# GLA scores as two half-row products per direction in two PSUM banks, with both spreads of q on ScalarE

## The chip, the cores and the metric

The kernel runs on one core of one Trainium2 chip. The metric is the device time of one execution in microseconds. Five engines work side by side: TensorE (PE; its weight loads are listed apart as PEld), VectorE (DVE), ScalarE (ACT), GpSimd (POOL) and SyncE (SP), which issues most of the DMAs. An engine runs its own instructions in the order in which they were written out and waits on semaphores for the others.

## What is computed

Two layers work on 1024 latent and 256 context tokens, 1280 in all, of width 1024. In each layer one input projection feeds four mixers: GLA (gated linear attention), neighbourhood attention (NA), a diagonal state space model (S5) and pooling. Their outputs go through gates and one output projection. The change touches GLA alone, which has 4 heads with keys of 32 and values of 64 and runs over the tokens forward and backward; the two results are added:

```python
def step(state, inp):
    qc, kc, vc, gc = inp
    b = jnp.cumsum(gc, axis=-2)
    diff = b[:, :, :, None, :] - b[:, :, None, :, :]
    decay = jnp.exp(jnp.where(lower[:, :, None], diff, -jnp.inf))
    att = jnp.einsum('bhid,bhjd,bhijd->bhij', qc, kc, decay)
    o = (jnp.einsum('bhij,bhje->bhie', att, vc)
         + jnp.einsum('bhid,bhde->bhie', qc * jnp.exp(b), state))
    b_last = b[:, :, -1:, :]
    state = (jnp.exp(b_last)[:, :, 0, :, None] * state
             + jnp.einsum('bhjd,bhje->bhde', kc * jnp.exp(b_last - b), vc))
    return state, o
...
o + flip_seq(gla_chunked(flip_seq(qh), flip_seq(kh), flip_seq(vh), flip_seq(log_gate(gb, 1)), s_b))
y = o * lax.rsqrt(jnp.mean(o * o, axis=-1, keepdims=True) + NORM_EPS) * g
```

`att` is what this document calls the scores: for each head a product over its 32 key channels.

## The kernel before

**Tiling.** The 4 heads' 32 key channels lie side by side on the 128 partitions, so that QF and KF (forward) and QB and KB (backward), with the decay already worked into them, are tiles of 128 channels by 1280 tokens. GLA goes over the tokens in chunks of 128, of which there are ten. Layer 0 needs scores for all ten. Layer 1 is the last, needs no output for the 256 context tokens, and makes scores for eight, so 18 chunks have scores.

**The two loops.** `gla` first runs the backward loop. For each chunk it scales the state into `glSb` (L1040, VectorE) and updates the state: a transpose of KB on TensorE (L934), a copy to `kt` on ScalarE (L936), a product with `vt` on TensorE (L938), and two VectorE operations (L1031 to `km`, L1032 to `S`). Then the forward loop runs. For each chunk:

- The spread (`gla_spread`): to keep the heads apart in one product over all 128 partitions, q is written four times side by side into `qs` [128, 4, 128], and in copy h the channels of the other heads are set to zero. The forward q is spread by four ScalarE instructions (L971), the backward q by one GpSimd instruction over 512 columns (L973).
- The scores (L1062): one matmul for each direction, K as the weights and 512 columns of `qs` streaming, into one bank of PSUM from the pool `pb`. All of it is float32, which TensorE runs in two passes, so each matmul stands in the profile as two.
- The masks, both VectorE, PSUM to SBUF: the forward scores times a mask into `at` (L1065), then the backward ones over it where they belong (L1067).
- `gla_finish`: forward state times QF (L946), `at` times `vt` for four heads (L948), backward state times QB (L950), all into one bank; a square on ScalarE (L953), a sum (L955), an inverse square root in a row of [128, 4] operations (L132 to L140) and a scaling (L957) on VectorE, two transposes on TensorE (L960), a copy out on ScalarE (L962) and a DMA.
- The forward state's update (L934 to L938, L1031, L1032).

**What sets the order.** GLA, the S5 projection, NA's projections (L318, L334), the modulation (L198) and later the pooling's projection and the gates are written one after the other, the latter three marked as later. A scheduler with priorities works out each engine's order when the kernel is built: where GLA waits for another engine, TensorE is given matmuls of the later work, which this document calls fillers. Pools set what can be open at once: `pb` has 5 banks of PSUM in GLA, `qs` two buffers, `at` two. After S5, a branch splits the program; no filler crosses it. The other way of computing GLA behind that branch isn't executed.

Of the kernel before, what the change touches and what calls it, by code (L numbers as in the profile page):

```python
# [50 lines left out]
BD = 'ap'  # L51
ATB = 2
QSB = 2
# [17 lines left out]
class Kernel:  # L71
# [893 lines left out]
    def gla_spread(self, out, Q, ind, d):  # L965

        nc = self.nc
        sh = [128, 4, 128]
        if BD[d] == "a":
            for h in range(4):  # L970
                nc.scalar.activation(out[:, h], Q, AF.Copy, scale=ind[:, h:h + 1])  # L971
        else:
            (nc.gpsimd if BD[d] == "p" else nc.vector).tensor_tensor(out, Q.unsqueeze(1).to_broadcast(sh), ind.unsqueeze(2).to_broadcast(sh), ALU.mult)  # L973

    BWD = [1, 0] + list(range(NT - 1, 1, -1))

    def gla(self, l, last):
# [7 lines left out]
        with self.phase("glF", True):  # L985
# [28 lines left out]
            with self.phase("glm"):  # L1014
# [3 lines left out]
                ind = self.t([128, 4], "ind1", 1)  # L1018
# [33 lines left out]
                for c in range(NT):  # L1052
                    cs = slice(c * 128, (c + 1) * 128)
                    vt = self.gla_load_v(l, c)
                    if not (last and c < 2):
                        at = self.t([128, 4, 128], "at", ATB)
                        sh = [128, 4, 128]
                        for d, (K, Q) in enumerate(((KF, QF), (KB, QB))):
                            qs = self.t(sh, "qs", QSB)
                            self.gla_spread(qs, Q[:, cs], ind, d)  # L1060
                            ps = self.pb()
                            nc.tensor.matmul(ps, lhsT=K[:, cs], rhs=qs.rearrange("p h i -> p (h i)"), start=True, stop=True)  # L1062
                            pv = ps.rearrange("p (h i) -> p h i", h=4)
                            if d == 0:
                                v.tensor_tensor(at, pv, mf.unsqueeze(1).to_broadcast(sh), ALU.mult)  # L1065
                            else:
                                v.copy_predicated(at, mb.unsqueeze(1).to_broadcast(sh), pv)  # L1067
                        sf = turned(S, 0, c, self.t([128, 256], "Sft", 2))
                        self.gla_finish(l, c, vt, lambda h: at[:, h, :], QF[:, cs], sf, QB[:, cs], Sb[:, c, :], gn)
                    if c != NT - 1:  # L1070
                        S = state(0, KF, vt, c, S)
# [444 lines left out]
    def run(self):  # L1516
# [9 lines left out]
        for l in range(DEPTH):  # L1526
# [5 lines left out]
            with self.phase("mods", True) as pool:  # L1532
# [3 lines left out]
                self.npb = 5  # L1536
# [44 lines left out]
def _consts():  # L1581
# [33 lines left out]
    out["ind1"] = (ind > 0).astype(f)  # L1615
# [110 lines left out]
```

## Time and profile before

| | us |
|---|---|
| median of 3 runs | 1388.77 |
| the runs | 1386.04 to 1389.81 |
| the profiled execution | 1390.5 |
| its span in the trace | 1388.7 |

| engine | busy us | share of the span |
|---|---|---|
| PE | 1265.2 | 91% |
| DVE | 912.5 | 66% |
| ACT | 584.9 | 42% |
| POOL | 203.8 | 15% |

GLA's two loops run from about 228 to 366 us in layer 0 and from about 930 to 1047 us in layer 1. A wait of TensorE there adds to the time unless a later wait swallows it; a wait of another engine does so only where TensorE then waits for it. In the timelines below a group's length holds the modelled end of its last pass; what a pass takes is read from the start of one group to the start of the next.

### The profile page before, as it was taken

To read this page: it belongs to the slowest core of one execution; us is meant where nothing else is said; L and a number is where in the kernel's file an instruction comes from. 1 tells how busy PE (TensorE), PEld (TensorE's weight loads), DVE (VectorE), ACT (ScalarE), POOL (GpSimd) and SP (SyncE) were. 2 spreads that over 40 slices of the span, in tenths; PEclk is the share of its full clock that TensorE was granted. 3 is DMA by queue.
4 is the path that set the end of the run, shared out by engine and by line. 5 is a ranking of instruction groups with operands and counts; after the bars stand their busy time and mean duration, and the time that the engine had idled before them with its cause. 6 is when DMAs were issued, how large, how long until landed. Compare 5 with 4: busy or idle time off the path is not lost. (4 is left out here: it accounts for less than half of the span.)

```text
span 1388.7 us, 20066 instructions
## 1 busy us (share of the span) xinstructions
PE 1265.2 (91%) x6958; PEld 1011.0 (73%) x6958; DVE 912.5 (66%) x2269; ACT 584.9 (42%) x1218; POOL 203.8 (15%) x212
## 2 busy tenths in 40 slices
PE   5799999999999999988989999999899998777897
PEld 2698967667777678767878989768667776665676
DVE  2777577456388548773866787586654884776383
ACT  2653443223333347663555644443323333665321
POOL 0100000001100024351410000000112100234220
PEclk9699999999999999999999999999999999998999
DMA  9436685752533267746832475865215535754662
GB/s 330 157 116 224 192 252 166 217 182 76 164 127 113 81 184 197 209 141 208 246 124 92 124 230 188 246 183 157 79 46 185 166 108 161 201 150 139 192 210 91
DMA packets 223477, 231.07 MB, mean 166 GB/s; under 512 B 47016, under 2 KB 176552, under 8 KB 223040
## 3 DMA queue, kind: packets, MB, share of 16 engines
q1 hardware_dynamic: 221776, 227.14, 53.8%
q10 hardware_dynamic: 1584, 2.49, 0.5%
q8 instruction: 58, 0.95, 0.3%
q14 instruction: 59, 0.48, 0.1%
HBM read 159.97 MB, written 69.62 MB: 165 GB/s over the span
## 5 line engine op out<-in xcount | busy, mean ns | idle before, releaser
L318 PE MATMUL pa<-ahi,wh 128*128 128x512 f32 (+1 forms) x664 | 171.7, 387 | 5.0 <-ACT stg L1407 2.1
L318 PE MATMUL pa<-alo,wh 128*128 128x512 f32 (+1 forms) x664 | 166.9, 380 | 0.1
L318 PE MATMUL pa<-ahi,wl 128*128 128x512 f32 (+1 forms) x664 | 165.1, 377 | 0.1
L318 PEld LDWEIGHTS pa<-ahi,wh 128*128 128x128 f32 x664 | 116.0, 193 | 31.8 <-issue 6.4
L318 PEld LDWEIGHTS pa<-alo,wh 128*128 128x128 f32 x664 | 115.7, 192 | 25.7 <-issue 7.9
L318 PEld LDWEIGHTS pa<-ahi,wl 128*128 128x128 f32 x664 | 115.6, 191 | 23.5 <-issue 5.5
L334 PE MATMUL pa<-wh,ahi 128*128 128x256 f32 (+1 forms) x480 | 83.4, 305 | 5.8 <-ACT wh L302 2.4
L303 POOL TENSOR_TENSOR wl<-w,wh 128x1024 fp32r<-128x1024 f32 (+1 forms) x19 | 46.3, 2441 | 286.0 <-PE pa L318 170.8
L388 PE MATMUL po<-wx,ahi 128*128 128x512 f32 x312 | 79.8, 396 | 1.1 <-DVE stg L474 1.0
L334 PE MATMUL pa<-wl,ahi 128*128 128x256 f32 (+1 forms) x480 | 79.6, 299 | 0.1
L1315 PE MATMUL nS<-naK,naQ 128*128 128x256 f32 (+2 forms) x256 | 61.2, 359 | 19.8 <-DVE nast L1322 17.8
L302 ACT CAST wh<-w 128x1024 fp32r<-128x1024 f32 (+1 forms) x51 | 53.8, 1057 | 58.8 <-PE pa L318 36.4
L334 PEld LDWEIGHTS pa<-wh,ahi 128*128 128x128 f32 x480 | 68.8, 197 | 11.4 <-issue 3.3
L334 PE MATMUL pa<-wh,alo 128*128 128x256 f32 (+1 forms) x480 | 76.0, 294 | 0.0
L334 PEld LDWEIGHTS pa<-wl,ahi 128*128 128x128 f32 x480 | 68.1, 195 | 6.6 <-issue 5.3
L1315 PEld LDWEIGHTS nS<-naK,naQ 128*128 128x128 f32 x256 | 46.0, 209 | 32.9 <-DVE nast L1322 28.1
L388 PEld LDWEIGHTS po<-wx,ahi 128*128 128x128 f32 x312 | 59.2, 191 | 14.7 <-DVE stg L474 1.4
L334 PEld LDWEIGHTS pa<-wh,alo 128*128 128x128 f32 x480 | 65.7, 193 | 5.7 <-issue 5.5
L1322 DVE CUSTOM_DVE_ANT_0 naP<-nS,nab 128x640 f32<-128x640 f32 (+1 forms) x64 | 50.3, 787 | 24.3 <-PE nS L1315 12.0
L1327 ACT ACTIVATE naP<-naP,nast 128x640 f32<-128x640 f32 (+1 forms) x64 | 51.5, 805 | 25.1 <-DVE nast L1322 22.3
L1382 PE MATMUL nT<-naPT,naV 128*128 128x256 f32 (+3 forms) x368 | 53.4, 284 | 7.9 <-DVE naPT L1367 5.4
L973 POOL TENSOR_TENSOR qs<-QB,ind 128x512 f32<-128x512 f32 x18 | 19.2, 1066 | 275.4 <-PE pb L1062 159.8
(395 smaller groups left out, 2601.6 us busy)
## 6 DMA issues: line engine op xcount, KB each, us to landing
wm<-in_w_mod_dram SPq DMA_DIRECT2D x48, 512.0 KB
w<-in_w_in_dram SPq DMA_DIRECT2D x41, 512.0 KB
s5R<-dR SPq DMA_DIRECT2D x16, 960.0 KB
xt<-in_tok_dram SPq DMA_DIRECT2D x20, 512.0 KB
dR<-sp_R SPq DMA_DIRECT2D x16, 512.0 KB
dG<-stg SPq DMA_DIRECT2D x32, 256.0 KB
w<-in_w_out_dram SPq DMA_DIRECT2D x16, 512.0 KB
naQ<-dQ SPq DMA_DIRECT2D x24, 320.0 KB
```

What stands on the lines that cost most here:

```text
L302: nc.scalar.copy(hi, raw)
L303: (next(engines) if engines else self.eng(2)).tensor_tensor(lo, raw, hi.bitcast(F32), ALU.subtract)
L318: nc.tensor.matmul(ps[:, :t1 - t0], lhsT=w(k), rhs=x[:, k, t0:t1], start=(i == 0), stop=(i == 23))
L334: nc.tensor.matmul(ps[:, :n], lhsT=x[:, k, t * 128:(t + 1) * 128], rhs=w(k), start=(i == 0), stop=(i == 23))
L388: self.nc.tensor.matmul(o, lhsT=x[:, k], rhs=m(k), start=first and i == 0, stop=last and i == len(todo) - 1)
L973: (nc.gpsimd if BD[d] == "p" else nc.vector).tensor_tensor(out, Q.unsqueeze(1).to_broadcast(sh), ind.unsqueeze(2).to_broadcast(sh), ALU.mult)
L1315: nc.tensor.matmul(ps[:, c * 128:(c + n) * 128], lhsT=Qb[:, i, :], rhs=K[:, b * 128:(b + n) * 128], start=(i == 0), stop=(i == 1))
L1322: v.tensor_tensor_reduce(P[:, 0:nk], ps, bias[:, b0:b0 + nk], 1.0, -NEG, ALU.add, ALU.min, nm)
L1327: nc.scalar.activation(P[:, 0:nk], src, AF.Exp, bias=nm, scale=-1.0, accum_out=l1)
L1382: nc.tensor.matmul(out[:, q:q + n], lhsT=w, rhs=x, start=(i == 0), stop=(i == len(todo) - 1))
```

## The change

The heads are taken in two halves of TensorE's rows: heads 0 and 1 on partitions 0 to 63, heads 2 and 3 on partitions 64 to 127. `qs` becomes [128, 2, 128]: copy 0 keeps the even head of each half, copy 1 the odd one. A direction's scores are then two matmuls (L1059), one for each half: 64 rows of K as the weights, 256 columns of `qs` streaming, at rows 0 and 64 of the array. The two halves write to different banks of one new tile `sc` [128, 1024], which has a single buffer; each bank holds the forward and the backward scores of two heads. The masks (L1064, L1065) are still two VectorE operations, now over both banks. Both directions are spread by ScalarE (L967), two instructions each, so four a chunk as before; GpSimd has no spread left. `pb` has 3 banks in GLA where it had 5, which makes room for `sc`.

```diff
-BD = 'ap'
...
-    def gla_spread(self, out, Q, ind, d):
-
-        nc = self.nc
-        sh = [128, 4, 128]
-        if BD[d] == "a":
-            for h in range(4):
-                nc.scalar.activation(out[:, h], Q, AF.Copy, scale=ind[:, h:h + 1])
-        else:
-            (nc.gpsimd if BD[d] == "p" else nc.vector).tensor_tensor(out, Q.unsqueeze(1).to_broadcast(sh), ind.unsqueeze(2).to_broadcast(sh), ALU.mult)
+    def gla_spread(self, out, Q, ind):
+
+        for h in range(2):
+            self.nc.scalar.activation(out[:, h], Q, AF.Copy, scale=ind[:, h:h + 1])
...
-                ind = self.t([128, 4], "ind1", 1)
+                ind = self.t([128, 2], "ind1", 1)
...
-                        sh = [128, 4, 128]
+
+                        ps = self.ps2.tile([128, 1024], F32, tag="sc", bufs=1, name=self.nm("sc"))
+                        pd = ps.rearrange("p (b d n) -> p d b n", b=2, d=2)
                         for d, (K, Q) in enumerate(((KF, QF), (KB, QB))):
-                            qs = self.t(sh, "qs", QSB)
-                            self.gla_spread(qs, Q[:, cs], ind, d)
-                            ps = self.pb()
-                            nc.tensor.matmul(ps, lhsT=K[:, cs], rhs=qs.rearrange("p h i -> p (h i)"), start=True, stop=True)
-                            pv = ps.rearrange("p (h i) -> p h i", h=4)
-                            if d == 0:
-                                v.tensor_tensor(at, pv, mf.unsqueeze(1).to_broadcast(sh), ALU.mult)
-                            else:
-                                v.copy_predicated(at, mb.unsqueeze(1).to_broadcast(sh), pv)
+                            qs = self.t([128, 2, 128], "qs", QSB)
+                            self.gla_spread(qs, Q[:, cs], ind)
+                            for b in range(2):
+                                hp = slice(64 * b, 64 * b + 64)
+                                nc.tensor.matmul(pd[:, d, b], lhsT=K[hp, cs], rhs=qs[hp].rearrange("p h i -> p (h i)"), start=True, stop=True)
+                        av = at.rearrange("p (b h) i -> p b h i", b=2)
+                        sh = [128, 2, 2, 128]
+                        every = lambda m: m.unsqueeze(1).unsqueeze(1).to_broadcast(sh)
+                        pv = pd.rearrange("p d b (h i) -> p d b h i", h=2)
+                        v.tensor_tensor(av, pv[:, 0], every(mf), ALU.mult)
+                        v.copy_predicated(av, every(mb), pv[:, 1])
...
-                self.npb = 5
+                self.npb = 3
...
-    out["ind1"] = (ind > 0).astype(f)
+    out["ind1"] = (ind[:, 0:2] + ind[:, 2:4] > 0).astype(f)
```

Line numbers of the kernel after are a few smaller: L933, L935 and L937 are the transpose, the copy and the product of the state's update (L934, L936 and L938 before), L945, L947 and L949 the three products of `gla_finish`, L959 its transposes, L317, L333 and L197 the fillers.

The scheduler moves work. TensorE in the backward loop of layer 0, before: the updates' pairs L938 and L934 with fillers L334 (`pa`) between them, then the first chunk's scores.

```order
L938 MATMUL pb_1801<-vt_1795,kt_1799 128x256
L934 MATMUL pb_1810<-c_ident,KB_1563 128x128
L334 MATMUL pa_3261<-wl_3205,ahi 128x256
L334 MATMUL pa_3261<-wl_3211,ahi 128x256 x3
L938 MATMUL pb_1814<-vt_1808,kt_1812 128x256
L934 MATMUL pb_1823<-c_ident,KB_1563 128x128
L334 MATMUL pa_3261<-wl_3211,ahi 128x256
L334 MATMUL pa_3261<-wh_3204,alo 128x256 x3
L938 MATMUL pb_1827<-vt_1821,kt_1825 128x256
L1062 MATMUL pb_1842<-qs_1837,KF_1561 128x512
L1062 MATMUL pb_1847<-qs_1845,KB_1563 128x512
L946 MATMUL pb_1852<-Sft_1850,QF_1560 128x256
```

TensorE there now. `sc` are the half-row scores, of the first chunk and then of the second.

```order
L937 MATMUL pb_1725<-vt_1719,kt_1723 128x256
L933 MATMUL pb_1732<-c_ident,KB_1563 128x128
L1059 MATMUL sc_1837<-qs_1838,KF_1561 128x256
L937 MATMUL pb_1736<-vt_1730,kt_1734 128x256
L933 MATMUL pb_1745<-c_ident,KB_1563 128x128
L1059 MATMUL sc_1837<-qs_1838,KF_1561 128x256
L937 MATMUL pb_1749<-vt_1743,kt_1747 128x256
L933 MATMUL pb_1758<-c_ident,KB_1563 128x128
L1059 MATMUL sc_1837<-qs_1843,KB_1563 128x256 x2
L317 MATMUL pa_3172<-ahi,wh_3098 128x512 x2
L317 MATMUL pa_3172<-alo,wh_3098 128x512 x7
L937 MATMUL pb_1762<-vt_1756,kt_1760 128x256
```

The scores of the first chunks have moved up among the updates, in the places of fillers, and the two halves of a direction are in part apart.

ScalarE in the same loop, before: `kt` are the copies that the updates need, `qs` the forward spreads, of which the first chunk's come ahead of the loop and the next after it.

```order
L936 COPY kt_1734<-pb_1732 128x128
L936 COPY kt_1747<-pb_1745 128x128
L936 COPY kt_1760<-pb_1758 128x128
L936 COPY kt_1773<-pb_1771 128x128
L1199 CAST stn_3197<-pa_3172 128x8x8x8
L936 COPY kt_1786<-pb_1784 128x128
L936 COPY kt_1799<-pb_1797 128x128
L1218 CAST stg_3241<-pa_3216 128x4x64
L936 COPY kt_1812<-pb_1810 128x128
L936 COPY kt_1825<-pb_1823 128x128
L971 ACTIVATE qs_1895<-QF_1560,ind_361_1713 128x128 x4
```

ScalarE there now.

```order
L967 ACTIVATE qs_1838<-QF_1560,ind_361_1713 128x128 x2
L967 ACTIVATE qs_1843<-QB_1562,ind_361_1713 128x128 x2
L935 COPY kt_1734<-pb_1732 128x128
L935 COPY kt_1747<-pb_1745 128x128
L967 ACTIVATE qs_1896<-QF_1560,ind_361_1713 128x128 x2
L935 COPY kt_1760<-pb_1758 128x128
L967 ACTIVATE qs_1901<-QB_1562,ind_361_1713 128x128 x2
L935 COPY kt_1773<-pb_1771 128x128
L935 COPY kt_1786<-pb_1784 128x128
L967 ACTIVATE qs_1956<-QF_1560,ind_361_1713 128x128 x2
L935 COPY kt_1799<-pb_1797 128x128
L967 ACTIVATE qs_1961<-QB_1562,ind_361_1713 128x128 x2
```

Both directions' spreads of the next chunks stand between the copies `kt`.

TensorE around the scores of one chunk in layer 1, before.

```order
L318 MATMUL pa_14236<-ahi,wl_14231 128x512 x3
L938 MATMUL pb_12459<-vt_12405,kt_12457 128x256
L1062 MATMUL pb_12473<-qs_12468,KF_11991 128x512
L1062 MATMUL pb_12478<-qs_12476,KB_11993 128x512
L334 MATMUL pa_13710<-wh_13436,ahi 128x256
L334 MATMUL pa_13710<-wl_13431,ahi 128x256 x2
L946 MATMUL pb_12483<-Sft_12481,QF_11990 128x256
```

TensorE around one chunk's scores there now.

```order
L333 MATMUL pa_13680<-wh_13430,ahi 128x256
L1059 MATMUL sc_12588<-qs_12589,KF_11991 128x256 x2
L1059 MATMUL sc_12588<-qs_12594,KB_11993 128x256 x2
L333 MATMUL pa_13680<-wh_13430,ahi 128x256 x3
L333 MATMUL pa_13680<-wh_13436,ahi 128x256 x4
L333 MATMUL pa_13680<-wl_13431,ahi 128x256 x3
L959 MATMUL pb_12449<-c_ident,sq_12430 128x128 x2
L933 MATMUL pb_12455<-c_ident,KF_11991 128x128
```

The four half-row products of a chunk stand in one group between full-array fillers (L333), with the transposes of the chunk before (L959) after them.

## Rows read from the trace of the kernel before

**Rows 1.** section 1 of the page: busy us (share of the span) x instructions

```profile
PE 1265.2 (91%) x6958; PEld 1011.0 (73%) x6958; DVE 912.5 (66%) x2269; ACT 584.9 (42%) x1218; POOL 203.8 (15%) x212
```

**Rows 2.** busy time by stretch (us), engine by engine, then granted clock, DMA share

```profile
231.00:249.00 18.00, 18.00 (x98) 13.85 (x98) 12.30 (x29) 4.24 (x14) 0.00 (x0) 1.00 0.62 170
985.00:1011.00 26.00, 20.07 (x94) 14.39 (x93) 15.98 (x38) 9.23 (x22) 6.80 (x4) 0.98 0.37 105
1011.00:1047.00 36.00, 34.67 (x148) 24.79 (x147) 16.29 (x57) 9.08 (x21) 4.46 (x3) 0.96 0.17 50
```

**Rows 3.** what TensorE waited for, 224 to 366 us: total, times, longest us

```profile
PE pb L946 <- DVE Sft L1040: 1.9, 1, 1.9
PE pb L960 <- DVE sq L957: 1.4, 4, 0.8
```

**Rows 4.** the same, 930 to 1047 us

```profile
PE pb L960 <- DVE sq L957: 5.8, 7, 2.4
PE pa L318 <- ACT stg L1407: 2.1, 2, 1.4
```

**Rows 5.** timeline, TensorE, 248 to 252 us: start, length, line, tile, passes

```profile
248.35 1.02 PE L1062 MATMUL pb<-qs,KF 128*128 128x512 f32 x2
249.21 1.02 PE L1062 MATMUL pb<-qs,KB 128*128 128x512 f32 x2
250.07 0.59 PE L946 MATMUL pb<-Sft,QF 128*128 128x256 f32 x2
250.60 1.05 PE L198 MATMUL pm<-wm,csil 128*32 128x512 f32 x4
251.58 0.86 PE L334 MATMUL pa<-wh,alo 128*128 128x256 f32 x5
```

**Rows 6.** timeline, TensorE, the end of the first block in layer 1

```profile
1173.48 1.98 PE L318 MATMUL pa<-ahi,wl 128*128 128x512 f32 x8
1175.31 0.63 PE L1315 MATMUL nS<-naK,naQ 128*128 128x512 f32 x2
```

**Rows 7.** timeline, TensorE, 277 to 279 us

```profile
277.79 1.07 PE L198 MATMUL pm<-wm,csil 128*32 128x512 f32 x8
278.79 0.62 PE L334 MATMUL pa<-wl,ahi 128*128 128x256 f32 x3
```

**Rows 8.** timeline, TensorE, 463 to 465 us

```profile
463.71 0.49 PE L318 MATMUL pa<-ahi,wl 128*128 128x512 f32 x1
464.14 0.71 PE L810 MATMUL pb<-c_ident,s5yc 64*128 64x64 f32 x8
```

**Rows 9.** VectorE by line, 231 to 249 us: busy us, mean ns, idle before

```profile
L1031 DVE SCALAR_TENSOR_TENSOR km<-pb,glsm,bmask 128x256 f32<-128x256 f32 x8 | 3.9, 482 | 3.7 <-PE pb L938 3.5
L1032 DVE SCALAR_TENSOR_TENSOR S<-S,glsm,km 128x256 f32<-128x256 f32 x7 | 3.4, 480 | 0.1
L1040 DVE TENSOR_SCALAR glSb<-S,glsm 128x256 f32<-128x256 f32 x8 | 2.8, 344 | 0.1
```

**Rows 10.** the two mask lines: ns min/median/max, first and last start

```profile
L1065 DVE TENSOR_TENSOR at<-pb,mF x18: 677/683/691, 249.6 to 1033.1; 128x512 f32<-128x512 f32 x18
...
L1067 DVE COPY_PREDICATED at<-mB,pb x18: 716/730/754, 250.5 to 1034.0; 128x512 f32<-128x512 int32 x18
```

**Rows 11.** ScalarE by line, 231 to 249 us

```profile
L936 ACT COPY kt<-pb 128x128 f32<-128x128 f32 x8 | 2.1, 266 | 9.5 <-PE pb L934 9.5
```

**Rows 12.** the tile qs: instructions, ns min/median/max, first and last start

```profile
L971 ACT ACTIVATE qs<-QF,ind x72: 385/387/403, 227.9 to 1024.2; 128x128 f32<-128x128 f32 x72
...
L973 POOL TENSOR_TENSOR qs<-QB,ind x18: 1040/1042/1222, 228.0 to 1024.2; 128x512 f32<-128x512 f32 x18
```

**Rows 13.** timeline, all engines, 994 to 997 us

```profile
994.09 2.37 POOL L303 TENSOR_TENSOR wl<-w,wh 128x1024 fp32r<-128x1024 f32 x1 [5.26 <-ACT wh L302]
994.12 2.35 DVE L138 TENSOR_TENSOR grw<-gry 128x4 f32<-128x4 f32 x1
...
996.50 0.16 DVE L139 TENSOR_TENSOR grw<-grw,grv 128x4 f32<-128x4 f32 x1
```

## The prediction

> **What bounds the kernel now.** I read the page's busy times first: TensorE works 91% of the span [rows 1], so the question is what the change does to TensorE's own work and to its waits. Then the busy time by stretch: the backward loop of layer 0 has TensorE busy for 18.00 of 18 us, while the forward loop of layer 1 leaves 5.9 us idle in one stretch of 26 and runs the next at a granted clock of 0.96 [rows 2]. Then who TensorE waited for there: 3.3 us in layer 0 and 7.9 us in layer 1, nearly all for VectorE's chain through L957, for the state L1040 and for ScalarE's L1407 [rows 3, 4]. None of these names the spreads. Then the timeline around one chunk's scores, which gives their price on TensorE: from the first L1062 at 248.35 to L946 at 250.07 are 1.72 us, four passes of 512 columns at 0.43 [rows 5], so 0.215 for 256 columns. Last the end of the first block of layer 1: fillers without a gap up to 1175.31 [rows 6]. What the scheduler moves out of GLA's loops is done there, at the same price. So moving fillers neither wins nor loses; work and waits of TensorE in front of it do.
>
> **Term 1, the columns: −12.9 us.** Before: 18 chunks of 1.72 us, 31.0 us. Now a direction is two products on different rows of the array, each two passes of 256 columns. If the halves run side by side, a chunk takes four slots of 0.215, 0.86 us. No tiles side by side by rows are in this trace; the nearest rows have them side by side by columns: eight L198 passes of 512 columns on 128*32 tiles go from 277.79 to 278.79, two slots of 0.43 and 0.14 over, so four tiles did run at once [rows 7]. I take full overlap where the halves stand next to each other. In the order they don't always: the first three chunks of each layer have a half by itself in several places, which makes 84 slots in all instead of 72. 84 x 0.215 = 18.1, and 18.1 − 31.0 = −12.9. The other end is no overlap, 31.0 us as before, so 0.
>
> **Term 2, going in and out of the half-row tiles: +11.2 us.** Each time TensorE goes from full-array matmuls to half-row ones and back it loses something. Going in or out: one L318 pass between two groups of half-row L810 takes 0.43 us from start to start [rows 8], where a run of eight takes 1.83, or 0.23 each [rows 6]: 0.20 for one change. The other change: four L198 passes on two tiles, two slots of 0.43, take 0.98 from start to the next L334 [rows 5], 0.12 over; the eight in [rows 7] 0.14 over. To this I add 0.07 for weights that can't be loaded behind the matmul before, a part of what the same rows show. So 0.40 for a round trip; from 0.25 (if the 0.14 is nearly all) to 0.50 (0.20 twice, and 0.10 for the weights). In the order after the change I count 28 such trips, 15 in layer 0 and 13 in layer 1, since the split chunks make two to four each and the other twelve one each. 28 x 0.40 = 11.2; the ends are 7.0 and 14.0. Terms 1 and 2 together: −1.7 us, a gain of 0.46 for each of the twelve chunks that stand together (1.72 − 0.86 − 0.40) and a loss for the split ones.
>
> The Trainium skill ("TensorE: Matmul & The Clock Gate", Part 3, on what overlaps) says that matmuls start and end in program order and only weight loads are pulled ahead. Written as first half pass one and two, then second half pass one and two, only neighbours would overlap. The rows for the eight L198 passes speak against it: they would take five slots of 0.43, over 2.1 us, and took 1.00 [rows 7]. The same part's table gives 3.07 times for four row tiles at once, not 4; as an estimate by that share a chunk would take 1.1 us instead of 0.86, and the sum would be some 3 us higher. No run here shows row tiles yet.
>
> **Term 3, the backward loop: +2 us.** Before, a step of it had fillers between the transpose and the product, and TensorE lost nothing [rows 2]. Now the scores of two or three chunks stand there in each layer. VectorE's part of a step is L1031 0.48, L1032 0.48 and L1040 0.34, 1.30 us [rows 9], and each chunk's masks add 0.68 + 0.73 = 1.41 [rows 10]. Over the six densest steps of a layer that is 6 x 1.30 + 2 x 1.41 = 10.6 us. TensorE has there six products and transposes (6 x 0.55), some 2.6 to 3.0 of scores, six trips at 0.40 and 1.7 to 2.1 of fillers: 10.4 us. Two engines that need each other's results and are equally full wait in turns. Besides, `kt` (0.27 us [rows 11]) now queues behind two spreads of 0.387 [rows 12] on ScalarE, and L937 waits for it: 0.12 + 0.77 + 0.27 + 0.43 = 1.59 for a step, against 1.38 of TensorE's own work without fillers, 0.2 lost in each of some ten steps. I take +2. The lower end is 0, if the fillers next to it cover the gaps; the upper is four spreads ahead of a copy in six steps: 1.55 + 0.27 + 0.55 = 2.37, less 1.38, six times, +6.
>
> **Term 4, GpSimd and VectorE: −1 us.** GpSimd loses 18 spreads of 1.04 us [rows 12]. Nobody in [rows 3, 4] waited for them, so this wins nothing by itself. But GpSimd also makes `wl` (L303), and the trace shows it and VectorE in each other's way: L303 from 994.09 for 2.37 us, and VectorE's tiny L138 from 994.12 for 2.35, where its like L139 takes 0.16 [rows 13]. TensorE's longest waits, 2.4 and 1.9, are of this size; all that waited for L957 in layer 1 and for L1040 in layer 0, 5.8 + 1.9, is the most that such meetings can have cost [rows 3, 4], and the lower clock of 0.96 over 36 us behind them costs up to 1.4 more [rows 2]. In the new order `wl` follows casts that stand right beside L952's squares on ScalarE, so one meeting in layer 0 and one or two in layer 1 are to be expected again. From 0 to −4 (about half of those 9.1); I take −1.
>
> **At nothing.** ScalarE's spreads: 72 before, 72 now, of the same 128x128. The masks: as many elements, as many instructions; a pattern over two banks that cost up to 0.04 more each (as far as 0.716 and 0.754 lie apart [rows 10]) would lie behind TensorE's fillers. `pb` with 3 banks: in the forward loop at most three are open at once. The single `sc`: a chunk's first product waits for the masks of the chunk before, 1.41 us of VectorE, with a chunk's fillers between; in the backward loop it is part of term 3. No DMA is added or taken away.
>
> **Sum.** −12.9 + 11.2 + 2 − 1 = −0.7 us. Against the profiled execution of 1390.5 that is 1389.8; that execution lies 1.7 above the median, so against the median 1388.77 it is **1388.1**. With all bounds at their good ends (−12.9 + 7.0 + 0 − 4) 1378.9, at their bad ends (−12.9 + 14.0 + 6 + 0) 1395.9.
>
> **Rivals.** *Cheap trips.* If a trip costs 0.25, because weights of the second half load behind the first, and the meetings of term 4 mostly miss: −12.9 + 7.0 + 1 − 3 = −7.9, **1380.9**. For it: L198's trips come out near 0.14 for one change; against it: the 0.20 of L318 between half-row groups. 0.32. *The halves run in turn.* Then the columns stay at 31.0 and the trips come on top: +11.2 + 2 − 1 = +12.2, **1401.0**, slower. It decides wherever a half's matmul starts only when the other half's has ended; no row here shows row tiles at once, and the column tiles speak against it. 0.11. *The backward loop is bound by ScalarE's copies.* Term 3 at +6 and term 4 at 0: +4.3, **1393.1**, slower; its point is a copy `kt` queued behind four spreads. For it is the order of ScalarE; against it, that fillers do stand between some steps. 0.13. *Only neighbours overlap*, as in the rule on program order but as a mechanism here: a group of four products takes five slots instead of four, 12 x 0.215 = +2.6, **1390.7**. 0.04.
>
> **How the numbers follow.** A measurement of this kernel can tell some 0.3% from no change, 4.2 us: below 1384.6 is faster, above 1392.9 slower. The forecast's case has 0.40, of which 0.36 within 0.3% and 0.02 on either side. Cheap trips 0.32 are faster; halves in turn 0.11 slower; the backward loop 0.13, of which 0.09 slower and 0.04 within; neighbours 0.04 within. So faster 0.34, within 0.44, slower 0.22. The range 1379 to 1396 takes in both ends of the sum; left out are the halves in turn (0.11) and some 0.07 of cheap trips.
>
> **What would show it.** L1059's passes of two halves should start within some 0.01 us of each other and a group of four should take about 0.86 us plus 0.4 to the next full-array pass; in turn would show 1.72. TensorE's busy time between 225 and 300 us should fall short by waits for `kt` or km of 1 to 3 us. L303's successor should still meet one VectorE chain of L132 to L140 in each layer with a 2.4 us operation. I am wrong if groups of L1059 take 1.2 us or less in all (cheap trips), or if TensorE's waits in the backward loops are over 5 us.

## The result and the profile after

The changed kernel takes 1406.72 us (median of 4 runs, 1402.54 to 1411.36) where the kernel before took 1389.29 beside it: a ratio of 1.0119, with a 95% interval from 1.0092 to 1.0145. It is slower by some 17 us, outside the range that was predicted. Its profiled execution took 1402.54 us with a span of 1400.6, so the two traces, of 1388.7 and 1400.6 us, show 12 of the 17.

The page's busy times after the change, answering [rows 1]: TensorE has 7 us more busy time, GpSimd 19 less than its 203.8.

```profile
PE 1272.5 (91%) x7030; PEld 1018.0 (73%) x7030; DVE 916.4 (65%) x2269; ACT 584.7 (42%) x1218; POOL 184.7 (13%) x194
```

The new scores are what the prediction said they would be. The timeline of TensorE after the change, answering [rows 5] (start, length, line, tile, passes):

```profile
251.21 0.48 PE L1059 MATMUL sc<-qs,KF 64*128 64x256 f32 x1
251.21 0.48 PE L1059 MATMUL sc<-qs,KB 64*128 64x256 f32 x1
251.53 0.38 PE L1059 MATMUL sc<-qs,KF 64*128 64x256 f32 x1
251.53 0.80 PE L1059 MATMUL sc<-qs,KB 64*128 64x256 f32 x3
...
254.10 0.73 PE L317 MATMUL pa<-ahi,wl 128*128 128x512 f32 x2
254.76 0.70 PE L1059 MATMUL sc<-qs,KF 64*128 64x256 f32 x4
255.30 0.60 PE L1059 MATMUL sc<-qs,KB 64*128 64x256 f32 x4
255.83 0.51 PE L317 MATMUL pa<-ahi,wl 128*128 128x512 f32 x1
```

Half-row passes start in pairs, in the same hundredth of a microsecond (251.21, 251.53). A chunk's eight passes go from 254.76 to 255.83, 1.07 us, which is four slots of 0.215 and 0.21 over: the first slot after the change of tiles and the last before the next change are each some 0.1 longer. So are the full-array passes on either side of a change. The two L317 passes ahead take 0.66 where two take 0.46, but half of that belongs to the change out of L197's 128*32 tiles in front of them; behind the chunk at 995.72 the first L317 pass takes 0.34 where one takes 0.23. A change of tiles costs 0.20, a round trip 0.41, and a chunk 1.27 us, where it cost 1.72.

The backward loop of layer 0, answering the first of [rows 2], is still full, and in GLA of layer 0 TensorE waits 3.0 us where it waited 3.3 [rows 3]. The first row is busy time from 234 to 250 us (TensorE, its loads, VectorE, ScalarE, GpSimd, clock, DMA share), the others are TensorE's waits from 224 to 366 us (total, times, longest):

```profile
234.00:250.00 16.00, 16.00 (x70) 10.17 (x68) 12.15 (x29) 6.67 (x21) 0.00 (x0) 1.00 0.57 162
```

```profile
PE pb L959 <- DVE sq L956: 2.7, 6, 1.0
...
PE pb L945 <- DVE Sft L1034: 0.3, 1, 0.3
```

The 12 us appear later. These are the starts of the same TensorE work in timelines of both kernels, of a second execution of the changed kernel (a_repeat) and of three others that come below:

| us from the start | before | after | a_repeat | a_wl0 | a_wl1 | a_wlv1 |
|---|---|---|---|---|---|---|
| last chunk's forward product, GLA of layer 0 | 352.0 | 347.9 | 347.2 | 346.9 | 346.0 | 343.7 |
| first NA scores, layer 0 | 500.8 | 504.8 | 507.4 | 498.6 | 503.4 | 494.3 |
| last output product, layer 0 | 759.8 | 759.7 | 764.0 | 748.2 | 761.4 | 745.0 |
| last chunk's forward product, GLA of layer 1 | 1034.5 | 1035.0 | 1041.7 | 1024.7 | 1037.6 | 1019.6 |
| first NA scores, layer 1 | 1175.3 | 1185.2 | 1188.2 | 1171.2 | 1176.6 | 1160.1 |
| end | 1388.7 | 1400.6 | 1405.6 | 1385.6 | 1389.0 | 1371.9 |

GLA of layer 0 ends 4 us sooner, S5 behind it gives 8 back (in part fillers that GLA no longer holds), and layer 0 ends where it did. In layer 1 it is S5 again, between GLA's end and the first NA scores: 140.8 us before, 150.2 after. Busy time and granted clock in four stretches of layer 1, up to the end of its first block, before:

```profile
889.50:930.00 40.50, 39.56 (x176) 26.29 (x175) 39.14 (x71) 19.20 (x26) 0.00 (x0) 1.00 0.74 210
930.00:952.00 22.00, 21.93 (x152) 18.42 (x150) 11.11 (x29) 6.82 (x19) 1.04 (x1) 1.00 0.59 169
952.00:1047.00 95.00, 86.29 (x421) 64.40 (x421) 52.67 (x161) 26.87 (x68) 14.39 (x10) 0.98 0.29 84
1047.00:1175.30 128.30, 120.22 (x580) 92.06 (x579) 87.54 (x145) 47.01 (x91) 12.59 (x7) 0.99 0.48 156
```

And after:

```profile
889.50:934.00 44.50, 41.16 (x179) 28.03 (x179) 37.90 (x71) 19.91 (x27) 0.00 (x0) 0.97 0.71 203
934.00:953.00 19.00, 17.91 (x90) 10.46 (x85) 12.26 (x25) 7.04 (x21) 0.00 (x0) 0.98 0.55 161
953.00:1047.00 94.00, 86.69 (x494) 69.71 (x495) 51.39 (x166) 26.20 (x69) 6.13 (x3) 0.98 0.28 83
1047.00:1187.10 140.10, 129.89 (x596) 98.61 (x595) 90.61 (x148) 47.66 (x90) 13.64 (x8) 0.94 0.47 148
```

TensorE's idle time in these 285.8 and 297.6 us is 17.8 and 22.0, 4.2 more. A stretch times one minus its clock is what the clock took: 3.2 us before, 12.0 after, 8.8 more (the clock is given to two digits, so give or take 1). Of the 11.8 us that the stretch grew that leaves 1.2 less, TensorE's own work, as forecast. In this trace the loss is waits and, twice as much, the clock.

The second trace of the same kernel, with every engine's order the same, puts the loss elsewhere. S5 of layer 1 takes 146.5 us there, at a clock of 0.98:

```profile
1041.70:1188.20 146.50, 135.35 (x640) 102.62 (x639) 92.90 (x161) 50.22 (x95) 14.94 (x8) 0.98 0.43 141
```

Its 16.9 us are 4.2 up to the end of layer 0, 3.0 up to the end of GLA in layer 1, 5.7 in S5 and 4.0 behind. What both traces share is the sum over the whole execution: TensorE's idle time is 123.5 us before, 128.1 and 131.6 after, and by the mean clocks of 0.968, 0.963 and 0.961 the clock took 44, 52 and 55. The page's busy times of a_repeat:

```profile
PE 1274.0 (91%) x7030; PEld 1019.8 (73%) x7030; DVE 916.0 (65%) x2269; ACT 584.6 (42%) x1218; POOL 184.7 (13%) x194
```

In S5 of layer 1 both traces have the same waits. They name one chain; the first row is before, the others are after:

```profile
PE pb L789 <- DVE s5x L779: 7.4, 4, 2.4
```

```profile
PE pb L788 <- DVE s5x L778: 5.1, 3, 2.5
PE pb L789 <- DVE s5x L778: 4.1, 2, 2.1
```

What stretches that chain stands in the timeline. Before:

```profile
1105.35 2.40 POOL L303 TENSOR_TENSOR wl<-w,wh 128x1024 fp32r<-128x1024 f32 x1 [17.53 <-PE pa L318]
1105.88 0.69 DVE L347 SCALAR_TENSOR_TENSOR stg<-stg,pa 128x512 f32<-128x512 f32 x1 [0.35 <-ACT stg L346]
1106.48 1.98 DVE L772 TENSOR_TENSOR_SCAN s5st<-rho,s5x 128x159 f32<-128x159 f32 x2
...
1111.07 0.49 PE L789 MATMUL pb<-s5R,s5x 128*128 128x128 f32 x2 [1.35 <-DVE s5x L779]
```

And after:

```profile
1111.06 0.42 DVE L778 TENSOR_TENSOR s5x<-s5v,s5x 64x256 f32<-64x256 f32 x1
...
1111.61 2.61 POOL L302 TENSOR_TENSOR wl<-w,wh 128x1024 fp32r<-128x1024 f32 x1 [18.58 <-PE pa L317]
...
1112.01 2.49 DVE L778 TENSOR_TENSOR s5x<-s5v,s5x 64x256 f32<-64x256 f32 x1
...
1114.55 0.49 PE L789 MATMUL pb<-s5R,s5x 128*128 128x128 f32 x2 [2.06 <-DVE s5x L778]
```

GpSimd's subtraction for the gates' weights meets VectorE in both kernels. Before, the first to start beside it was L347, which reads PSUM and isn't stretched, so only the scans behind it lost some 1.1 us. After, it met L778, the last step in front of a TensorE product: 2.49 us where the same line takes 0.42 half a microsecond earlier. TensorE then waits 2.06 us, and behind this wait, and behind the next such one, it is granted the lower level of 1.2 GHz for part or all of the stretch (busy times after the change, with the clock third from the end):

```profile
1115.00:1125.00 10.00, 10.00 (x38) 7.66 (x37) 7.49 (x15) 1.14 (x3) 0.00 (x0) 0.66 0.52 177
1140.00:1145.00 5.00, 5.00 (x18) 3.57 (x17) 4.88 (x11) 0.39 (x1) 0.00 (x0) 0.50 0.01 2
```

The change brings no more subtractions into S5. From 350 us to the first NA scores of layer 0 six start in either kernel, from 1040 us to those of layer 1 six as well; they only fall at other steps.

### The profile page after: what moved, and what is told of

Same layout as the page of the kernel before. It is cut to its first block, busy times and chain, and to the rows that moved or that the text cites. A ratio compares the mean times of both kernels' runs of the same rounds, so it can differ in the third digit from the quotient of the medians.

```text
span 1400.6 us, 20155 instructions
## 1 busy us (share of the span) xinstructions
PE 1272.5 (91%) x7030; PEld 1018.0 (73%) x7030; DVE 916.4 (65%) x2269; ACT 584.7 (42%) x1218; POOL 184.7 (13%) x194
## 3 DMA queue, kind: packets, MB, share of 16 engines
q10 hardware_dynamic: 1584, 2.49, 0.5%
## 5 line engine op out<-in xcount | busy, mean ns | idle before, releaser
L317 PE MATMUL pa<-ahi,wh 128*128 128x512 f32 (+1 forms) x664 | 171.3, 387 | 7.6 <-DVE stg L346 4.1
L317 PE MATMUL pa<-alo,wh 128*128 128x512 f32 (+1 forms) x664 | 168.9, 386 | 0.1
L317 PE MATMUL pa<-ahi,wl 128*128 128x512 f32 (+1 forms) x664 | 162.6, 374 | 0.0
L317 PEld LDWEIGHTS pa<-ahi,wh 128*128 128x128 f32 x664 | 116.7, 196 | 31.8 <-issue 5.4
L317 PEld LDWEIGHTS pa<-alo,wh 128*128 128x128 f32 x664 | 119.0, 196 | 27.8 <-issue 8.3
L317 PEld LDWEIGHTS pa<-ahi,wl 128*128 128x128 f32 x664 | 115.6, 190 | 23.8 <-issue 4.8
L333 PE MATMUL pa<-wh,ahi 128*128 128x256 f32 (+1 forms) x480 | 82.5, 305 | 7.9 <-ACT wh L301 2.4
L333 PE MATMUL pa<-wl,ahi 128*128 128x256 f32 (+1 forms) x480 | 80.3, 300 | 0.9 <-DVE wl L302 0.8
L333 PEld LDWEIGHTS pa<-wh,ahi 128*128 128x128 f32 x480 | 68.3, 197 | 17.6 <-issue 6.7
L333 PE MATMUL pa<-wh,alo 128*128 128x256 f32 (+1 forms) x480 | 77.0, 296 | 0.0
L333 PEld LDWEIGHTS pa<-wl,ahi 128*128 128x128 f32 x480 | 68.6, 197 | 5.7 <-issue 3.8
L333 PEld LDWEIGHTS pa<-wh,alo 128*128 128x128 f32 x480 | 66.3, 192 | 2.6 <-issue 2.0
L197 PE MATMUL pm<-wm,csil 128*32 128x512 f32 x192 | 49.0, 649 | 10.7 <-DVE nr2v L131 9.9
```

Of the source, the lines that this page charges most:

```text
L197: nc.tensor.matmul(state[0][32 * k:32 * k + 32, :], lhsT=self.csil[:, (k0 + k) // 2, 2 * (k % 2):2 * (k % 2) + 32], rhs=ws[k // 2][:, k % ...
L317: nc.tensor.matmul(ps[:, :t1 - t0], lhsT=w(k), rhs=x[:, k, t0:t1], start=(i == 0), stop=(i == 23))
L333: nc.tensor.matmul(ps[:, :n], lhsT=x[:, k, t * 128:(t + 1) * 128], rhs=w(k), start=(i == 0), stop=(i == 23))
```

## The experiments

Each kernel was timed beside the kernel before, on the same chip; the ratio is to those runs. Names beginning with a_ start from the changed kernel, with b_ from the one before.

| kernel | median us | ratio | 95% interval |
|---|---|---|---|
| a_repeat | 1404.19 | 1.0097 | 1.0063 to 1.0131 |
| a_full | 1404.52 | 1.0094 | 1.0059 to 1.0128 |
| a_zero | 1369.80 | 0.9856 | 0.9824 to 0.9888 |
| b_zero | 1373.43 | 0.9885 | 0.9851 to 0.9918 |
| a_wlv | 1380.52 | 0.9927 | 0.9900 to 0.9953 |
| b_wlv | 1388.28 | 0.9992 | 0.9971 to 1.0012 |
| a_pool | 1394.34 | 1.0033 | 1.0008 to 1.0057 |
| b_banks | 1390.88 | 1.0004 | 0.9982 to 1.0026 |
| a_wl1 | 1399.05 | 1.0060 | 1.0036 to 1.0083 |
| a_wl0 | 1385.72 | 0.9973 | 0.9957 to 0.9990 |
| a_wlv1 | 1374.05 | 0.9884 | 0.9861 to 0.9908 |
| b_wlv1 | 1383.32 | 0.9946 | 0.9921 to 0.9971 |
| a_qs3 | 1404.71 | 1.0121 | 1.0080 to 1.0163 |
| a_at3 | 1399.63 | 1.0085 | 1.0061 to 1.0108 |
| a_at1 | 1394.38 | 1.0039 | 1.0019 to 1.0059 |
| b_qs1 | 1409.18 | 1.0140 | 1.0103 to 1.0177 |

### The half rows, or the order and the meetings?

The changed kernel as it is, a_repeat.

> The changed kernel again, for its spread and a second trace. In the first trace TensorE lost against the kernel before 4 us more in waits of layer 1 and, by the granted clock (0.94 against 0.99 from 1047 us to the end of the first block), some 8 us more at half clock. Theory M (meetings): GpSimd's L302 happens to run into VectorE's S5 chain of layer 1 at worse places than before; then the same three long VectorE operations of 2.5 to 3.0 us stand in S5 again and the time is 1402 to 1411 us. Theory H (half rows): the half-row products themselves cost it. Theory O (order): the order of the fillers after the change costs it. H and O expect 1402 to 1411 too; this run only gives the spread.

It was slower by 0.6 to 1.3%, and its trace has the same waits in S5 of layer 1, 5.1 and 4.1 us for s5x, at the clock of 0.98 shown above where the first trace had 0.94. So the clock that the first trace lost in that stretch doesn't follow from these waits alone.

a_full:

```diff
-hp = slice(64 * b, 64 * b + 64)
+hp = slice(0, 128)
```

> The changed kernel, its four score products taken over all 128 rows instead of 64 (so the scores mix heads, which is another result); every engine's order is that of the changed kernel, word for word, but there are no half-row tiles, no trips in and out of them and no two products at once. By the prediction's terms 1 and 2 that is +12.9 - 11.2, about +1.7 us against the changed kernel. Theories M and O: 1402 to 1413 us, as the changed kernel. Theory H: back to 1388 to 1394, and the clock in S5 of layer 1 as before the change.

1404.52 beside a_repeat's 1404.19: no difference that can be told. Without half-row tiles, and with every engine's order the same, the whole loss stays. Theory H falls, and what is left is the order, with the spreads and the banks that make it. The 1.7 us that terms 1 and 2 give for the difference are smaller than these two intervals can tell.

a_zero and b_zero:

```diff
-(next(engines) if engines else self.eng(2)).tensor_tensor(lo, raw, hi.bitcast(F32), ALU.subtract)
+e = next(engines) if engines else self.eng(2)
+if e is nc.gpsimd:
+    e.memset(lo.bitcast(F32), 0.0)
+else:
+    e.tensor_tensor(lo, raw, hi.bitcast(F32), ALU.subtract)
```

> The changed kernel, GpSimd filling wl with zeros (a write without reads) where it subtracted wh from w, so the low part of the gates' weights is left out. Theory M: no VectorE operation in GLA and S5 is stretched to over 2 us any more, TensorE waits in S5 of layer 1 for under 4 us instead of 9.2, the clock there stays at 0.98 or more, and the time is 1380 to 1390, within 3 us of the same edit on the kernel before. Theories H and O: 12 to 17 us above the same edit on the kernel before.

> The kernel before with the same edit (GpSimd fills wl with zeros, the low part of the gates' weights is left out). Its own meetings cost it some 6 us of VectorE in S5 of layer 1 and 2.2 + 2.4 us of TensorE in GLA of layer 1. Theory M: 1380 to 1388 us, a gain of 2 to 8 over the kernel before; if meetings cost nothing on the way to the end, within 2 us of it.

The changed kernel lost 34 us by this, the kernel before 18, and the gap between them closed; if anything the changed one is now ahead. GpSimd's line in S5 of a_zero, and TensorE's waits from GLA's end in layer 1 to the first NA scores:

```profile
1093.25 0.95 POOL L304 MEMSET wl<- 128x1024 f32 x1 [19.07 <-PE pa L321]
```

```profile
PE pb L792 <- DVE s5x L782: 1.1, 3, 0.5
PE pb L793 <- DVE s5x L782: 0.2, 1, 0.2
```

The waits for s5x are 1.3 us instead of 9.2, and the granted clock of that stretch is 1.00. Both gains are larger than M expected. The edit takes away more than the meetings: the fill is 1.4 us shorter and waits neither for the cast nor for the load of w. Hence the next pair.

It also changes the order, because the scheduler makes a new one for every edit. By the longest common order of two traces, 386 of TensorE's 7030 instructions stand elsewhere in a_zero than in the changed kernel, 538 in a_wlv and 312 in a_wl0, which come below; in a_full all but two stand where they stood. On the kernel before, b_zero moves only 39 of 6958. So its 18 us are the price of the subtractions there (meetings, length and their waits together), while on the changed kernel meetings and order went at once.

### Was it the meetings, or the earlier wl?

a_wlv and b_wlv keep the subtraction and its inputs and put it on VectorE's own queue:

```diff
-self.proj_cols(l, 1824 + m0 * 128, 128, evac, chunks, psum=psum, engines=itertools.repeat(nc.gpsimd))
+self.proj_cols(l, 1824 + m0 * 128, 128, evac, chunks, psum=psum, engines=itertools.repeat(nc.vector))
```

> The changed kernel with the gates' wl made by VectorE (L302 on its own queue, 1.2 us each) where GpSimd made them in 2.4. With GpSimd filling zeros the changed kernel took 1369.8 us and the kernel before 1373.4, against 1404 and 1391 with the subtraction on GpSimd. Theory M (the meetings of GpSimd and VectorE are what the change lost by): 17 subtractions at 1.2 us come to VectorE in place of meetings at some 2.1, and wl again waits for its cast, so 1372 to 1388 us, and within 4 us of the same edit on the kernel before. Rival Z (filling zeros won because wl no longer waits for its cast and its DMA, not because the meetings are gone): 1395 to 1408 us, some 12 above the same edit on the kernel before.

> The kernel before with the gates' wl made by VectorE. Theory M: 1374 to 1388 us, below the kernel before by less than the changed kernel gains. Rival Z: within 5 us of the kernel before.

The changed kernel came from 1404 to 1380.5 with all of its work done: rival Z falls for it. On the kernel before the same edit won nothing that can be told. That is what rival Z forecast, not M; its trace has no long wait for s5x in layer 1 any more (0.9 us in all), but 9.1 us for the DMA of naQ at the first NA scores instead, and in layer 0 it ends no sooner. So the two kernels now differ by 0.65% the other way: in this pair, without subtractions on GpSimd, the changed kernel is ahead. That its 24 us are the meetings isn't shown: the edit moves 538 of TensorE's instructions, and on the other kernel, where it takes the meetings away as well, it won nothing.

### Which part of the change brings the meetings?

a_pool gives the backward spread back to GpSimd:

```diff
+if d == 0:
     for h in range(2):
         self.nc.scalar.activation(out[:, h], Q, AF.Copy, scale=ind[:, h:h + 1])
+else:
+    self.nc.gpsimd.tensor_tensor(out, Q.unsqueeze(1).to_broadcast(sh), ind.unsqueeze(2).to_broadcast(sh), ALU.mult)
```

> The changed kernel with the backward spread given back to GpSimd (one instruction over 256 columns). The scores stay in half rows, the banks stay, the order of every engine moves again. Theory M: the time follows where L302 then meets VectorE in S5 of layer 1; VectorE's operations that are stretched to over 2 us between 1040 and 1190 decide, anything from 1388 to 1408. Theory G (it was taking the spread from GpSimd, which lets L302 start earlier, that lost the time): back to 1386 to 1392.

b_banks gives the kernel before the new banks alone:

```diff
-self.npb = 5
+self.npb = 3
...
-ps = self.pb()
+ps = sc[:, d * 512:(d + 1) * 512]
```

> The kernel before with only the change's banks: its full-row scores go to the one buffer sc of two banks, pb has 3 banks; spreads as before. Theory B (three banks and a single score buffer are what moved the fillers and cost the time): 1398 to 1408 us. Theory M: the order moves a little, so 1386 to 1402 by where the meetings fall, with no relation to the half rows.

b_banks can't be told from the kernel before: theory B falls. Its trace has 7.8 us of waits for s5x in S5 of layer 1 and VectorE operations of 2.55 to 3.0 us beside four subtractions there, so such meetings alone don't tell a slow kernel from a fast one. a_pool lies 0.1 to 0.6% above, so two thirds of the loss went, and the rest stayed, with 8.5 us of waits for s5x. M's ranges were so wide that neither run could go against it. The banks alone don't make the loss. Whether taking the spread from GpSimd does (theory G) isn't settled: giving it back took most of the loss away and made another order, and no run moved the spread alone on the kernel before.

### Which layer?

a_wl0 (first) and a_wl1 (second) move the gates' wl to VectorE in one layer:

```diff
-engines=itertools.repeat(nc.gpsimd))
+engines=itertools.repeat(nc.gpsimd if l else nc.vector))
...
-engines=itertools.repeat(nc.gpsimd))
+engines=itertools.repeat(nc.vector if l else nc.gpsimd))
```

> The changed kernel with the gates' wl on VectorE in layer 1 alone. In the traces the changed kernel lost against the kernel before about 0 to 4 us up to the end of layer 0 and 10 to 12 in the first block of layer 1, and the edit on both layers took it from 1404 to 1380.5. Theory M with the loss placed in layer 1: TensorE waits for s5x under 2 us in layer 1's S5 instead of 9.2, the end of the first block comes 8 to 14 us sooner, 1390 to 1396 us. If layer 0's meetings matter as much: 1392 to 1398. Rival (all the gain of that edit comes out of layer 0): 1400 to 1408.

> The same in layer 0 alone. Theory M: layer 0's S5 loses its 4.1 us of waits for L346 and 3.6 for s5x, and the first output product of layer 0 comes 8 to 14 us sooner as with the edit in both layers, 1388 to 1396 us. Rival (layer 0's gain is absorbed by the wait for pooling at its end, as the 4 us that GLA gained there were): 1400 to 1408.

Layer 0's edit wins 1.24% (1.0097 to 0.9973, some 17 us), more than M expected. Layer 1's wins 0.37%, some 5, less than expected, and the intervals of a_repeat and a_wl1 overlap. I had put the loss in layer 1, where the first traces of the two kernels part. That was wrong: a_wl0 keeps all 9.2 us of waits for s5x in S5 of layer 1 and is still 0.1 to 0.4% faster than the kernel before. In a_wl1 the stretch from GLA's end to the first NA scores of layer 1 does shrink, from 150.2 us to 139.0, with the clock at 1.00. Its trace is of an execution of 1390.8 us, 8 below the median, so it can't say how much of that reaches the end:

```profile
1037.60:1176.60 139.00, 132.15 (x640) 100.62 (x640) 92.48 (x169) 51.48 (x97) 0.10 (x1) 1.00 0.45 149
```

```profile
PE nS L1313 <- DMA naQ<-dQ: 4.8, 1, 4.8
PE pa L317 <- ACT stg L1405: 0.7, 1, 0.7
PE pb L788 <- DVE s5x L778: 0.6, 3, 0.3
```

The waits for s5x went from 9.2 to 0.6 us; 4.8 came back as a wait for the DMA of naQ, the next in line.

In layer 0, S5 before, then after, then a_wl0:

```profile
PE pb L789 <- DVE s5x L779: 1.8, 3, 1.0
PE pb L790 <- DVE s5x L779: 1.6, 1, 1.6
PE pa L318 <- DVE stg L347: 1.5, 1, 1.5
```

```profile
PE pa L317 <- DVE stg L346: 4.1, 2, 2.7
PE pb L788 <- DVE s5x L778: 3.6, 3, 1.9
```

```profile
PE pv L737 <- DMA s5R<-dR: 1.7, 1, 1.7
PE pb L821 <- DVE s5g L816: 1.1, 1, 1.1
```

The waits that stretched VectorE operations bring, those for s5x, are 3.4 us before and 3.6 after. What is new is the wait for stg, and 2.7 of its 4.1 us aren't a meeting. On ScalarE, L1271 waits for the DMA of nab, and two L345 stand behind it, which read the banks that TensorE's next filler needs (after):

```profile
493.87 1.38 ACT L1271 ACTIVATE nab<-nab 128x1408 f32<-128x1408 f32 x1 [3.60 <-DMA nab<-in_na_bias_dram]
495.15 0.85 ACT L345 ACTIVATE stg<-pa 128x512 f32<-128x512 f32 x2
496.51 1.19 PE L317 MATMUL pa<-ahi,wh 128*128 128x512 f32 x4 [2.70 <-DVE stg L346]
```

Before, and in a_wl0, one such operation stands behind that wait and TensorE doesn't stop there. So a_wl0 takes away the meetings of layer 0 and, by its other order, this wait too.

And the end of layer 0, where TensorE waits for pooling, which is GpSimd's: before (2 rows), after, a_wl0.

```profile
PE nT L1460 <- POOL ps L1441: 4.2, 1, 4.2
PE nT L1460 <- POOL ps L1451: 2.5, 1, 2.5
```

```profile
PE nT L1458 <- POOL ps L1449: 4.1, 1, 4.1
```

```profile
PE nT L1458 <- DVE nay L1394: 3.9, 1, 3.9
```

Layer 0 ends 11.5 us sooner in a_wl0 than after the change (759.7 to 748.2 in the table above), 6.2 of them by the first NA scores. With the subtractions off GpSimd's queue, pooling is no longer what TensorE waits for, but a wait of 3.9 us for nay stands in its place; and in b_wlv, without subtractions on that queue too, a wait of 3.8 for pooling stays.

### A version that beats both

a_wlv1 also makes the two subtractions of the program's start on VectorE:

```diff
-SWE = 0
+SWE = 1
```

> The changed kernel with the gates' wl on VectorE in both layers and the two at the start too, whose GpSimd instruction (2.6 us each) stretches VectorE by 4.4 us in the first 100 us. Theory M: 0 to 5 us below the same without the start's edit (1380.5), so 1374 to 1381 us and faster than the kernel before. If the start waits for DMA anyway: 1379 to 1383.

b_wlv1 is the same edits on the kernel before.

> The kernel before with all of wl on VectorE, the start's too: the other half of the pair with the same edits on the changed kernel (1374.1 us). With the gates' alone the pair was 1380.5 against 1388.3, with zeros 1369.8 against 1373.4, so the change by itself is worth 4 to 8 us where GpSimd makes no wl. Theory M: 1378 to 1384 us. Rival (the start's edit is what made the changed kernel fast, and the change is worth nothing): 1372 to 1376.

a_wlv1 takes 1374.05 us, 1.2% below the kernel before (0.9 to 1.4%). Its counterpart, timed in another set beside the same kernel before, takes 1383.32. Between them lie 0.6%, about 9 us, in favour of the changed kernel where GpSimd makes no wl, and the rival about the start falls. The start's edit itself moves two of TensorE's instructions in either kernel, so with the order kept the two subtractions of the start cost some 6 us: 0.43% from a_wlv to a_wlv1, 0.46% from b_wlv to b_wlv1. The intervals of each two touch, but the two pairs agree.

### Chance of place, or inherent?

Three more orders of the changed kernel and one of the kernel before, by the number of buffers alone:

```diff
-QSB = 2
+QSB = 3
...
-ATB = 2
+ATB = 3
...
-ATB = 2
+ATB = 1
...
-QSB = 2
+QSB = 1
```

In this order a_qs3, a_at3, a_at1 and b_qs1.

> The changed kernel with three buffers for qs where it has two; few rows of the order move, on ScalarE above all. If the loss is chance of place: anywhere from 1385 to 1408 us, and the three nudged kernels lie over 5 us apart. If it is inherent in the change: 1400 to 1408, as the changed kernel.

> The changed kernel with three buffers for the masked scores where it has two. Chance of place: 1385 to 1408. Inherent: 1400 to 1408.

> The changed kernel with one buffer for the masked scores, so the scheduler can't move the next chunk's masks up, some 1 to 3 us more waits in GLA. Chance of place: 1385 to 1410. Inherent: 1401 to 1411.

> The kernel before with one buffer for qs, which puts the second spread behind the first product, so some waits more in GLA and another order behind it. Chance of place: the kernel before moves as much as the changed one does, 1383 to 1403. Inherent: 1388 to 1393, the waits alone.

The changed kernel moves between 0.4 and 1.2% above the kernel before by the number of buffers, so some 10 of its 17 us are chance of order; the fastest of these orders has one buffer fewer for the masked scores. But none of its orders with all of GpSimd's subtractions came below the kernel before. b_qs1 doesn't settle the other side: its trace shows TensorE waiting for GpSimd's spread itself (9 us in 16 waits in GLA of both layers), so its 1.4%, outside both of its ranges, isn't chance alone. What stays open is why some 5 us are common to all of the changed kernel's orders, and why b_wlv won nothing in layer 0. A hint for the first: in every trace of the changed kernel in which GpSimd makes layer 0's wl, S5 of layer 0 takes 155.7 to 160.2 us, against 148.8 in the kernel before and 147.6 in b_banks, and the wait for stg there is 4.1 to 4.7 us (155.8 and 3.7 in b_qs1, which is slow too).

## Why the prediction was wrong

**The step that failed** is the last of the first part: that what the scheduler moves out of GLA's loops is done in front of the first block's end "at the same price. So moving fillers neither wins nor loses". I counted the fillers' passes and not what a new order does to the waits behind GLA. a_full shows it: with the changed kernel's order, spreads and banks, and without half-row products, it takes 1404.5 us, 0.6 to 1.3% above the kernel before; the banks alone (b_banks) cost nothing that can be told. Which part of the new order does it, the fillers' or the spreads', no run parts. TensorE's idle time grew by 4.6 and 8.1 us in the two traces of the changed kernel, and what the clock took by about 8 and 10, in different places each time.

The loss goes when GpSimd's subtractions for the gates' weights go, those of layer 0 above all: without them the changed kernel takes 1380.5 (a_wlv), without layer 0's 1385.7 (a_wl0). How they bring it about isn't shown, and the cause stays open there. S5 holds as many of them as before. TensorE's waits for s5x went from 7.4 to 9.2 us in layer 1 and from 3.4 to 3.6 in layer 0, too little for 17, and a_wl0 is fast with the 9.2 in place. A wait of 2.7 us in layer 0 comes from ScalarE's order. And the runs that take the subtractions from GpSimd change the order too, which by the buffers alone moves this kernel by 0.8%. A pair with the order held fixed, as in a_full, would be needed to part them.

**Term 4** looked at the right mechanism and at GLA alone. There it came out about as said: in layer 1 3.2 us of waits for L956 where 5.8 stood in [rows 4], but 1.6 for Sft behind a meeting at 1012.33, 8.1 us of waits in all from 934 to 1047 against 8.7; in layer 0 no wait of 2 us. I had the row of a meeting [rows 13], its price, and that `wl` was to move; the same question for S5, 60 us on, would have given a rival on the slow side.

**Terms 1 and 2** held. Four slots of 0.215 for a chunk, both halves at once; 28 trips in the trace, as counted, at 0.41 for a round trip, forecast as 0.40. The rule of the Trainium skill ("TensorE: Matmul & The Clock Gate", Part 3) on program order, as the prediction applied it, and the 3.07 times for four row tiles in that part's table would have given a chunk, by estimate, 1.08 and 1.1 us of slots where 0.86 stand in the rows: where the halves stood together their passes started in pairs all through, and two row tiles were twice as fast as one. TensorE's own work in layer 1 came out 1.2 us less (give or take 1), for a forecast of 1.7 in both layers.

**Term 3** was too high: nothing in layer 0, and in layer 1's loop 0.5 us for km. ScalarE's spreads between the copies `kt` cost no wait that the profile names. Neither sign of being wrong that the prediction named came: a chunk takes 1.27 us with its trip, and no backward loop waits for 5.

**The rivals.** Cheap trips: no, the trip was 0.41. Halves in turn would have given 1401, near what came, and is wrong all the same, near by luck: the halves ran together, and the kernel that has no halves is as slow. The backward loop and the neighbours didn't happen. None of them was the cause; a cost of the new order behind GLA, which goes with GpSimd's subtractions, I had given no chance.

**The sign.** In two pairs without GpSimd's wl the changed kernel is ahead, by 0.65% (a_wlv and b_wlv) and 0.6% (a_wlv1 and b_wlv1), more than the −0.7 us forecast; in a third (a_zero and b_zero) the 0.3% can't be told from nothing. It isn't shown that the half rows won this: each pair is two orders, and orders alone move the time by as much. In a_wlv1 the NA of layer 0 starts at 494.3 us, in b_wlv1 at 504.2, and the terms don't hold that.

## What to carry to other kernels

When an edit moves filler work, counting its passes isn't enough: the new order has waits of its own downstream. One run with the order kept and the point of the edit taken out (a_full) tells at once whether the mechanism or the order made the difference; do it first, and take two traces before a loss is placed in a stretch. An operation on GpSimd that reads two tensors isn't free for VectorE beside it: move it to VectorE's own queue once, in both kernels. An edit that looked 1.2% slower was 0.6% faster in another setting, so a difference of under 1% here belongs to the setting as much as to the edit.

## What the runs showed of the hardware

GpSimd's 128x1024 subtraction takes 2.4 us, and VectorE's two-input operations on SBUF that started in its first half microsecond mostly took 1.9 to 2.2 us longer, however small they are (0.42 to 2.49, 0.16 to 2.35); beside the fill with zeros, 0.95 us from 1093.25 in a_zero, L776 took its 0.82 us. L347, whose second operand is in PSUM, ran its 0.69 us beside a subtraction. The Trainium skill ("SBUF — State Buffer", SBUF: two separate sides) says that VectorE operations with two SBUF inputs and GpSimd operations that read SBUF lock each other out for a whole instruction. These rows agree.

A wait of TensorE of 2.1 to 2.5 us was followed by a lower clock in some places and not in others: after 1114.55 the clock was 0.66 for 10 us, after the wait of 2.29 us at 1093.37 it stayed at 1.00, and in a_repeat the same wait of 2.06, at 1120.08, was followed by 1.00 up to 1142. What decides between them these traces don't show.

Some ten microseconds, 0.8% of this kernel, hang on the order that the scheduler makes of the same work: a_qs3 and a_at1 differ in nothing but the numbers of buffers for qs and for the masked scores. I had not expected that much.
